# Where split weights and the parts of four combinations begin in SBUF: multiples of 128 bytes, or 8 to 112 bytes past one

## The chip, the cores and the metric

One core of one Trainium2 chip runs the whole program. The metric is the device time of one execution in microseconds (us).

## The reference

A trunk of two layers on 512 tokens of width 1024. Layer 0 mixes with multi-head latent attention (MLA), layer 1 with gated linear attention (GLA); an MLP follows each.

```python
for i in range(DEPTH):                      # DEPTH = 2
    xn = rms_norm(x, norm_mix[i])
    mix = mla_mixer(xn, ...) if i % 2 == 0 else gla_mixer(xn, ...)
    x = x + mix
    x = x + sq_relu_mlp(rms_norm(x, norm_mlp[i]), mlp_w_up[i], mlp_w_down[i])
return rms_norm(x, final_norm)

def sq_relu_mlp(xn, w_up, w_down):          # (512,1024) x (1024,4096) x (4096,1024)
    return jnp.square(jax.nn.relu(xn @ w_up)) @ w_down
```

MLA projects x to low-rank latents, from these to 8 heads of queries, keys and values, and applies causal softmax attention. GLA projects to queries, keys, values and gates and runs a chunked recurrence with a data-dependent decay. All data are float32.

## The kernel before, in words

Each float32 operand of a product is split in two: a high part, rounded to the type `float32r` by a copy on ACT, and a low part, the rest, by a subtraction on DVE (`split`, L104 and L107). A product of two split operands is then three matmuls: high by high, high by low, low by high (`mm3`, L112 to L114). A TensorE matmul has a stationary operand, at most 128 columns that are loaded ahead of it (LDWEIGHTS, PEld in the profile), and a moving one, here mostly 256 or 512 columns that stream through.

Weights come from HBM on SP's queue into tiles called `wraw` (in the MLP also `comb`), two in turn. `piece` splits one into a pair of tiles `wh` and `wl`, of which there are three each in turn, each of at most 1024 floats per partition. Both tags are used for two more tiles, `w_kr` in MLA and `wa` in GLA. All these come from one pool `sb`, whose tiles lie in SBUF one behind the other in the order of their first use: `wraw`, `wh`, `wl`, the sets A and B (split activations), `tmp` and more. Ahead of it lies the pool `const`, with the gains, the residual `xT` and small tables. Behind it the stages open pools of their own, among them `fast` for the MLP. Two tiles are wider than their contents: `gains` has 176 floats for 87, `rtok` 48 for 4. With these widths every tile of the `wh`, `wl`, A, B and `fast` tags begins at a multiple of 512 bytes. The residual tiles begin 64 bytes past a multiple of 128.

The MLP (`mlp`) is done by blocks of 512 hidden columns. The first block goes through plain three-term products. The other seven are a scheme with seven products in place of eight, for `w_up` and for `w_down`: the activations and the weights are cut in quadrants, sums and differences of quadrants are formed, and results are added up. `quadrants` forms four combinations of activation quadrants once per MLP, T1 to T4, and splits each into a tile of 4 x 2 x 256 floats: for each of four k, the high and the low part. `step` does one block: seven up products (`up_product`, L936: stationary a split weight of 128 columns, moving a plain quadrant or a combination, 256 columns, 24 matmuls each) in turn with seven down products (`down_product`, L945: stationary the split hidden activations, moving a split weight of 512 columns, 12 matmuls each). Four of the seven up products of a block read a combination, three a plain quadrant, which is a slice of set A. Two MLPs with seven such blocks make 14 steps. A product begins when its weight is split; a `wh` or `wl` tile is written again three splits later.

In the other stages `a_type`, `b_type` and `out_start` call `mm3` with a split weight as the stationary or the moving operand. The order of instructions on an engine is that of the program text, apart from a few marked places; none of these is near the change.

Of the kernel before, what the change touches and what calls it, by code (L numbers as in the profile page):

```python
# [10 lines left out]
F32 = mybir.dt.float32  # L11
F32R = mybir.dt.float32r
# [6 lines left out]
P = 128  # L19
D = 1024  # L20
S = 512
NT = S // P
ND = D // P
FF = 4096
FB = 512
TH = S // 2
MH = 8
NOPE = 128
ROPE = 64
# [6 lines left out]
RANK = 16  # L36
# [14 lines left out]
def trunk_kernel(ctx: ExitStack, tc: tile.TileContext, t_in: dict, out: bass.AP):  # L51
# [3 lines left out]
    const = ctx.enter_context(tc.tile_pool(name="const", bufs=1))  # L55
    sb = ctx.enter_context(tc.tile_pool(name="sb", bufs=1))
    count = [0]

    def uname(s):
        count[0] += 1  # L60
        return f"{s}_{count[0]}"
# [14 lines left out]
    def bank(tag):  # L76
        return psum["pool"].tile([P, 512], F32, tag=f"ps_{tag}", bufs=psum["banks"][tag], name=uname("ps"))
# [24 lines left out]
    def split(src, hi, lo, hi_eng=ACT, lo_eng=DVE, order=lambda i: i):  # L102
        if hi_eng is ACT:
            order(ACT.activation(hi, src, AF.Copy))  # L104
        else:
            hi_eng.tensor_copy(hi, src)
        lo_eng.tensor_tensor(lo, src, f(hi), ALU.subtract)  # L107
# [30 lines left out]
    def load(src, a, n):  # L138
        raw = sb.tile([P, a, n], F32, tag="wraw", bufs=2, name=uname("wraw"))
        SP.dma_start(raw, src)  # L140
        return raw

    def piece(raw, a, n, order=lambda i: i):
        hi = sb.tile([P, a, n], F32R, tag="wh", bufs=3, name=uname("wh"))
        lo = sb.tile([P, a, n], F32R, tag="wl", bufs=3, name=uname("wl"))
        split(raw, hi, lo, order=order)
        return hi, lo

    def cut(pair, *idx):
        return tuple(t[idx] for t in pair)  # L150
# [2 lines left out]
    rope_es = ExitStack()  # L153
    rk = rope_es.enter_context(tc.tile_pool(name="rope_keep", bufs=1, reuse_waits="tile"))

    gains_room = const.tile([P, 176], F32, name="gains")
    gains = gains_room[:, : N_GAIN + NT + 32]
    pos_i = gains[:, N_GAIN : N_GAIN + NT].bitcast(I32)
    invf = gains[:, N_GAIN + NT :]
# [38 lines left out]
    def gcol(name, j):  # L198
        c = GAIN_COL[name] + j
        return gains[:, c : c + 1]  # L200
# [166 lines left out]
    def col_chunk(w2d, c0, n):  # L367
        return load(w2d[:, c0 : c0 + n].rearrange("(k p) n -> p k n", p=P), w2d.shape[0] // P, n)


    def mla(layer, nrm, first, pools):
# [36 lines left out]
        KH = ND // 2  # L408
        raw = sb.tile([P, ND, 256], F32, tag="wraw", bufs=2, name=uname("wraw"))
        wq = []  # L410
        for h in range(2):
            ks = slice(h * KH, (h + 1) * KH)
            SP.dma_start(raw[:, ks], w_in[:, :256].rearrange("(k p) n -> p k n", p=P)[:, ks])
            wq.append(piece(raw[:, ks], KH, 256))
        for j in range(2):
            p = bank("c")
# [10 lines left out]

        raw = col_chunk(w_in, 256, P)
        w = piece(raw, ND, P)
        p = bank("b")  # L430
        a_type(p, w, X)
# [2 lines left out]


        raw = col_chunk(w_in, QL + KL, ROPE)
        wr = sb.tile([P, ND, 2, ROPE], F32R, tag="wh", bufs=3, name="w_kr")
        ACT.activation(wr[:, :, 1, :], raw, AF.Copy)
        DVE.tensor_tensor(wr[:, :, 0, :], raw, f(wr[:, :, 1, :]), ALU.subtract)
        p = bank("b")  # L440
# [24 lines left out]
        for k in range(2):  # L465
            SP.dma_start(raw[:, k], w_ukv[:, k, :, NOPE:])
        wv = [piece(raw[:, k : k + 1].rearrange("p a h c -> p a (h c)"), 1, D) for k in range(2)]
        V = [[None, None] for _ in range(NT)]
        VP = []
# [13 lines left out]
        for t in range(NT):  # L483
            tk = slice(t * P, (t + 1) * P)
            for hf in range(2):
                p = bank("bc"[hf])
# [15 lines left out]
            if t == 1:  # L502
# [3 lines left out]
                for j in range(2):  # L506
                    y = tmp()
                    DVE.scalar_tensor_tensor(y, pkv[j], gcol("kvn", 2 * layer + j), r_kv, ALU.mult, ALU.mult)
                    hi, lo = (keep.tile([P, S], F32R, tag=f"ckv{j}{x}", name=f"ckv{j}{x}") for x in "hl")
# [22 lines left out]
        wa = piece(raw3[:, 0:2], 2, 512)  # L532
        wq = [cut(wa, slice(None), 0), cut(wa, slice(None), 1), wb]
        qs = []
        for t in range(NT):
            tk = slice(t * P, (t + 1) * P)
            p = bank("b")
# [70 lines left out]
        p = bank("c")[:ROPE]  # L608
# [187 lines left out]
    def mlp(layer, nrm, nxt=None):  # L796
# [3 lines left out]
        KH = ND // 2  # L800
        first, second = slice(0, TH), slice(TH, S)
        es = ExitStack()
        fast = es.enter_context(tc.tile_pool(name=f"fast{layer}", bufs=1, reuse_waits="tile"))
# [11 lines left out]
        def comb(i):  # L815
            return fast.tile([P, 2 * S], F32, tag=f"comb{i}", bufs=1, name=uname("comb"))

        def by_k(t, n):
            return t.rearrange("p (k n) -> p k n", k=n)
# [4 lines left out]
        def signed(src, hi, lo, sign):  # L824
            ACT.activation(hi, src, AF.Copy, scale=sign)
            DVE.scalar_tensor_tensor(lo, src, sign, f(hi), ALU.mult, ALU.subtract)
# [34 lines left out]
        def quadrants():  # L861
            lead, trail = range(KH), range(KH, ND)
            quad["11"] = [nrm.parts[k][:, :, first] for k in lead]
            quad["21"] = [nrm.parts[k][:, :, first] for k in trail]
            quad["22"] = [nrm.parts[k][:, :, second] for k in trail]
            t1, t2, t3, t4 = (by_k(comb(i), KH) for i in range(2, 6))
            for k in lead:
                g1, g2 = (gcol(nrm.g, nrm.g0 + j) for j in (k, k + KH))
                u, v = xT[k], xT[k + KH]
                ACT.activation(t3[:, k], u[:, second], AF.Copy, scale=g1)  # L870
                DVE.scalar_tensor_tensor(t3[:, k], v[:, second], g2, t3[:, k], ALU.mult, ALU.subtract)
                DVE.scalar_tensor_tensor(t2[:, k], u[:, first], g1, t3[:, k], ALU.mult, ALU.add)
                DVE.scalar_tensor_tensor(t4[:, k], v[:, first], g2, t2[:, k], ALU.mult, ALU.subtract)
                DVE.scalar_tensor_tensor(t1[:, k], v[:, second], g2, t2[:, k], ALU.mult, ALU.subtract)
            for name, t, sign in (("T2", t2, -1.0), ("T3", t3, 1.0), ("T1", t1, -1.0), ("T4", t4, -1.0)):
                parts = fast.tile([P, KH, 2, TH], F32R, tag=name, name=uname(name))
                signed(t, parts[:, :, 0], parts[:, :, 1], sign)
                quad[name] = [parts[:, k] for k in lead]

# [163 lines left out]

        up_first(Q[0])
        quadrants()
        if not nxt:
            residual()
# [58 lines left out]
        if nxt:  # L1106
            room = [parts_room[(turn[0] + k) % 4] for k in range(4)]
# [5 lines left out]
            for c in range(2):  # L1113
# [10 lines left out]
                for j, p in enumerate(ps_):  # L1124
                    if j % 2 == 0:
                        w = piece(last_raw[c][:, :, j * P : (j + 2) * P], 4, 256)
                    for k in range(4):
                        wh, wl = cut(w, slice(None), k, slice(j % 2 * P, (j % 2 + 1) * P))
# [65 lines left out]
    def gla(layer, nrm, vtag, ytag):  # L1194
# [82 lines left out]

        own = tmp((P, NT, P))
        DVE.tensor_tensor(own, nrm.rstd.rearrange("p (t c) -> p t c", t=NT), ident.unsqueeze(1).to_broadcast([P, NT, P]), ALU.mult)
        rtok = sb.tile([P, 48], F32, tag="rtok", name="rtok")[:, :NT]  # L1280
        DVE.reduce_sum(rtok, own, AX.X)


# [1 line left out]
        raw = tmp((P, ND, RANK))  # L1285
        ACT.dma_start(raw, w_in[:, 2 * DK + 2 * D :].rearrange("(k p) n -> p k n", p=P))
        R2 = 2 * RANK
        wa = sb.tile([P, ND, 3, 2, RANK], F32R, tag="wl", bufs=3, name="wa")
        raw3 = raw.unsqueeze(2).to_broadcast([P, ND, 3, RANK])
        ACT.activation(wa[:, :, :, 1, :], raw3, AF.Copy)  # L1290
        DVE.tensor_tensor(wa[:, :, :, 0, :], raw3, f(wa[:, :, :, 1, :]), ALU.subtract)
# [6 lines left out]
        p = bank("a")  # L1298
# [361 lines left out]
    turns = rope_turns()  # L1660

    O, begun = mla(0, nrm, w0, mla_pools)
    rope_es.close()
    n_mlp0 = Norm(ND, inv_dr, "mlp", 0)
# [17 lines left out]
    mlp(0, n_mlp0, n_mix1)  # L1682
    psum_layout(False)
    Y, begun = gla(0, n_mix1, "B", "B")
    n_mlp1 = Norm(ND, inv_dr, "mlp", ND)
    out_proj(t_in["gla_w_o"][0], Y, n_mlp1, begun)
# [23 lines left out]
def build(nc, shapes):  # L1710
    args = {}
    for name, (shape, dt) in shapes.items():
        args[name] = nc.dram_tensor(f"in_{name}_dram", shape, dt, kind="ExternalInput").ap()
    o = nc.dram_tensor("out_0_dram", (S, D), F32, kind="ExternalOutput").ap()
    with tile.TileContext(nc) as tc:
        trunk_kernel(tc, args, o)
# [22 lines left out]
```

## Time and profile before

| | |
|---|---|
| median of 3 runs | 1061.13 us (1060.65 to 1061.31) |
| profiled execution | 1061.1 us |
| its span, first to last instruction | 1059.4 us |
| TensorE (PE) busy | 1049.3 us, 99% of the span, 5966 matmuls |
| weight loads (PEld) busy | 918.3 us, 87% |
| DVE busy | 876.1 us, 83% |
| ACT busy | 698.4 us, 66% |
| POOL busy | 113.3 us, 11% |

The page gives the busy time of each engine, the chain of work that ended last, and the costliest groups of instructions by source line, with count, mean and what ended the idle time before them. In a group, `ps<-wh,set` means that the moving operand is `wh` and the stationary one `set`. The duration of a matmul there has a modelled end and is longer than the distance from one matmul to the next; that distance is read from the chain in order of time, where `2.87 PE ps L936 x24` says that 24 matmuls took 2.87 us from the first start to the next piece.

### The profile page before, as it was taken

The numbers are of one execution on the slowest core, as the hardware profiler recorded it, in microseconds if no ns is written. First come the engines' busy times: TensorE is split into PE (matmuls) and PEld (weight loads), VectorE is DVE, ScalarE is ACT, GpSimd is POOL, SyncE is SP. The second block draws the span as 40 slices with busy tenths as digits, with TensorE's granted clock in tenths as the row PEclk, the third lists the DMA queues.
The fourth block names the chain that finished last, engine by engine and source line by source line (L and its number), as shares of the span: only waits on it lengthen the run. The fifth ranks groups of instructions, "written<-read, shape, count | busy, mean of one in ns | idle before, by whom it ended". The sixth has DMA issues, their size and how long they took to land.

```text
span 1059.4 us, 15597 instructions
## 1 busy us (share of the span) xinstructions
PE 1049.3 (99%) x5966; PEld 918.3 (87%) x5966; DVE 876.1 (83%) x1339; ACT 698.4 (66%) x1074; POOL 113.3 (11%) x128
## 2 busy tenths in 40 slices
PE   9999999999999999999999999999999999999997
PEld 7888888889999999998888888878899999999985
DVE  7899977979889889888686498469889989989993
ACT  7667654577767767766345565665567777777784
POOL 7410011101101111000000000000011010010000
PEclk9999999999999999999999999999999999999999
DMA  7311234765976875842322221434486696696622
GB/s 230 90 50 41 80 95 144 238 180 146 232 189 146 223 198 142 218 151 88 90 80 80 80 80 60 120 100 136 114 239 142 173 252 144 173 246 146 168 81 80
DMA packets 120492, 149.97 MB, mean 142 GB/s; under 512 B 9344, under 2 KB 86144, under 8 KB 120288
## 3 DMA queue, kind: packets, MB, share of 16 engines
q1 hardware_dynamic: 95920, 117.76, 34.5%
q0 software_dynamic: 22400, 29.36, 17.5%
q10 hardware_dynamic: 2096, 1.84, 0.6%
q8 instruction: 47, 0.77, 0.3%
q14 instruction: 29, 0.24, 0.1%
HBM read 144.49 MB, written 4.19 MB: 140 GB/s over the span
## 4 chain that ended last, share of the span: by engine, by line
PE 96%; DVE 2%; ACT 2%; issue 0%; DMA 0%; ACTq 0%; SPq 0%; DVEq 0%
PE ps L936 26%; PE ps L945 25%; PE ps L112 11%; PE ps L114 11%; PE ps L113 10%; PE ps L1130 2%; PE ps L1385 2%; PE ps L135 1%; PE ps L1165 1%; PE ps L405 1%; PE ps L1512 1%; DVE wl L107 0%; PE ps L668 0%; PE ps L1435 0%; PE ps L664 0%
## 5 line engine op out<-in xcount | busy, mean ns | idle before, releaser
L945 PE MATMUL ps<-wh,set 128*128 128x512 f32 x784 | 258.7, 391 | 0.0
L107 DVE TENSOR_TENSOR wl<-wraw,wh 128x1024 fp32r<-128x1024 f32 x139 | 169.5, 1222 | 40.8 <-ACT wh L104 40.5
L104 ACT ACTIVATE wh<-wraw 128x1024 fp32r<-128x1024 f32 x139 | 145.9, 1053 | 82.3 <-PE ps L113 38.9
L945 PEld LDWEIGHTS ps<-wh,set 128*128 128x128 f32 x784 | 147.5, 188 | 28.7
L936 PE MATMUL ps<-T,wh 128*128 128x256 f32 x896 | 163.5, 283 | 0.0
L104 ACT ACTIVATE wh<-comb 128x1024 fp32r<-128x1024 f32 x112 | 118.7, 1060 | 67.4 <-PE ps L936 43.7
L945 PE MATMUL ps<-wl,set 128*128 128x512 f32 x392 | 153.7, 392 | 0.0
L107 DVE TENSOR_TENSOR wl<-comb,wh 128x1024 fp32r<-128x1024 f32 x112 | 136.8, 1221 | 20.4 <-ACT wh L104 19.4
L936 PEld LDWEIGHTS ps<-T,wh 128*128 128x128 f32 x896 | 143.3, 191 | 4.5
L936 PE MATMUL ps<-T,wl 128*128 128x256 f32 x448 | 127.0, 283 | 1.0 <-DVE wl L107 1.0
L936 PE MATMUL ps<-set,wh 128*128 128x256 f32 x672 | 122.6, 283 | 0.0
L936 PEld LDWEIGHTS ps<-set,wh 128*128 128x128 f32 x672 | 107.4, 191 | 3.2
L112 PE MATMUL ps<-set,wh 128*128 128x512 f32 x280 | 109.4, 392 | 0.6 <-ACT set L1554 0.3
L113 PE MATMUL ps<-set,wh 128*128 128x512 f32 x280 | 109.5, 392 | 0.0
L114 PE MATMUL ps<-set,wl 128*128 128x512 f32 x280 | 109.0, 390 | 0.0
L936 PE MATMUL ps<-set,wl 128*128 128x256 f32 x336 | 95.2, 283 | 0.0
L936 PEld LDWEIGHTS ps<-T,wl 128*128 128x128 f32 x448 | 85.8, 191 | 1.5 <-DVE wl L107 1.4
L945 PEld LDWEIGHTS ps<-wl,set 128*128 128x128 f32 x392 | 74.0, 189 | 11.6
L925 POOL DMA_DIRECT2D comb<-in_mlp_w_down_dram x28 | 33.7, 1204 | 423.9 <-DMA comb<-in_mlp_w_down_dram 145.4
L936 PEld LDWEIGHTS ps<-set,wl 128*128 128x128 f32 x336 | 64.3, 191 | 0.0
L112 PEld LDWEIGHTS ps<-set,wh 128*128 128x128 f32 x280 | 52.5, 188 | 12.7 <-ACT wh L104 0.9
L104 ACT ACTIVATE set<-set 128x512 fp32r<-128x512 f32 (+1 forms) x70 | 41.9, 603 | 31.4 <-PE ps L945 29.4
(395 smaller groups left out, 2034.9 us busy)
## 6 DMA issues: line engine op xcount, KB each, us to landing
comb<-in_mlp_w_down_dram SPq DMA_DIRECT2D x74, 512.0 KB, 5.2
wraw<-in_mlp_w_up_dram SPq DMA_DIRECT2D x32, 1024.0 KB, 6.2
comb<-in_mlp_w_down_dram POOLq DMA_DIRECT2D x28, 512.0 KB, 8.1
wraw<-in_gla_w_in_dram SPq DMA_DIRECT2D x12, 1024.0 KB, 5.2
comb<-in_mlp_w_up_dram SPq DMA_DIRECT2D x14, 512.0 KB, 3.6
comb<-in_mlp_w_up_dram POOLq DMA_DIRECT2D x14, 512.0 KB, 8.9
wraw<-in_mlp_w_up_dram POOLq DMA_DIRECT2D x14, 512.0 KB, 7.3
wraw<-in_mla_w_o_dram SPq DMA_DIRECT2D x4, 1024.0 KB, 4.7
```

The source lines that it names most:

```text
L104: order(ACT.activation(hi, src, AF.Copy))
L107: lo_eng.tensor_tensor(lo, src, f(hi), ALU.subtract)
L112: PE.matmul(psum, wh, xh, start=start, stop=False)
L113: PE.matmul(psum, wh, xl, start=False, stop=False)
L114: PE.matmul(psum, wl, xh, start=False, stop=stop)
L135: PE.transpose(psum, src, ident[: src.shape[0], : src.shape[0]])
L405: PE.matmul(p, w[:, i, j * P : (j + 1) * P], x, start=start, stop=stop)
L925: POOL.dma_start(t, q(b, *more), accum_op=ALU.add)
L936: PE.matmul(o, a_, x_, start=start and j == 0 and k == 0 and n == 0, stop=k == KH - 1 and n == 2, skip_group_check=True)
L945: PE.matmul(o, x_, w_, start=start and k == 0 and n == 0, stop=k == 1 and n == 2, skip_group_check=True)
L1130: PE.matmul(p, a, x, start=False, stop=k == 3 and n == 2, skip_group_check=True)
L1385: PE.matmul(p[:, t - t0], k[:, t * P : (t + 1) * P], moving[:, t], start=True, stop=True)
```

## The change

`wh` and `wl` tiles grow by 32 floats, and the weight in them begins 0, 2 or 4 floats (0, 8 or 16 bytes) from the tile's start, by a count of the tiles that the tag has handed out. `w_kr` and `wa` are taken in the same way. Each combination's tile grows by 32 floats too, and its parts begin 12 (T2), 4 (T3), 20 (T1) or 28 (T4) floats from its start: 48, 16, 80 and 112 bytes. The widths of `gains` and `rtok` fall to 112 and 16 floats, 256 and 128 bytes less per partition. The tiles themselves begin at multiples of 128 bytes, of 512 no longer everywhere: sets A and B still do. No instruction is added, removed or moved.

```diff
+    taken = {"wh": 0, "wl": 0}
+
+    def weight_room(tag, a, n):
+        first = 2 * (taken[tag] % 3)
+        taken[tag] += 1
+        t = sb.tile([P, 2 * S + 32], F32R, tag=tag, bufs=3, name=uname(tag))
+        return t[:, first : first + a * n].rearrange("p (a n) -> p a n", a=a)
+
     def piece(raw, a, n, order=lambda i: i):
-        hi = sb.tile([P, a, n], F32R, tag="wh", bufs=3, name=uname("wh"))
-        lo = sb.tile([P, a, n], F32R, tag="wl", bufs=3, name=uname("wl"))
+        hi, lo = (weight_room(tag, a, n) for tag in ("wh", "wl"))
         split(raw, hi, lo, order=order)
         return hi, lo
...
-    gains_room = const.tile([P, 176], F32, name="gains")
+    gains_room = const.tile([P, 112], F32, name="gains")
...
-        wr = sb.tile([P, ND, 2, ROPE], F32R, tag="wh", bufs=3, name="w_kr")
+        wr = weight_room("wh", ND, 2 * ROPE).rearrange("p k (r c) -> p k r c", r=2)
...
             for name, t, sign in (("T2", t2, -1.0), ("T3", t3, 1.0), ("T1", t1, -1.0), ("T4", t4, -1.0)):
-                parts = fast.tile([P, KH, 2, TH], F32R, tag=name, name=uname(name))
+                at = {"T2": 12, "T3": 4, "T1": 20, "T4": 28}[name]
+                room = fast.tile([P, KH * S + 32], F32R, tag=name, name=uname(name))
+                parts = room[:, at : at + KH * S].rearrange("p (k a t) -> p k a t", k=KH, a=2)
                 signed(t, parts[:, :, 0], parts[:, :, 1], sign)
...
-        rtok = sb.tile([P, 48], F32, tag="rtok", name="rtok")[:, :NT]
+        rtok = sb.tile([P, 16], F32, tag="rtok", name="rtok")[:, :NT]
...
-        wa = sb.tile([P, ND, 3, 2, RANK], F32R, tag="wl", bufs=3, name="wa")
+        wa = weight_room("wl", ND, 6 * RANK).rearrange("p k (r a c) -> p k r a c", r=3, a=2)
```

## The prediction

> **What bounds the kernel now.** I read the page first (busy time, then the chain that ended last), then the chain in order of time around one step of the MLP, then the engines' busy time over that step.
>
> ```profile
> PE 1049.3 (99%) x5966; PEld 918.3 (87%) x5966; DVE 876.1 (83%) x1339; ACT 698.4 (66%) x1074; POOL 113.3 (11%) x128
> PEclk9999999999999999999999999999999999999999
> PE 96%; DVE 2%; ACT 2%; issue 0%; DMA 0%; ACTq 0%; SPq 0%; DVEq 0%
> PE ps L936 26%; PE ps L945 25%; PE ps L112 11%; PE ps L114 11%; PE ps L113 10%; PE ps L1130 2%; PE ps L1385 2%; PE ps L135 1%; PE ps L1165 1%; PE ps L405 1%; PE ps L1512 1%; DVE wl L107 0%; PE ps L668 0%; PE ps L1435 0%; PE ps L664 0%
> ```
>
> TensorE at its full granted clock carries 96% of the chain, and almost all of that are matmuls that read a split weight: the up products (`up_product`, L936), the down products (`down_product`, L945) and the three-term products (`mm3`, L112 to L114). Transfers, ACT and DVE hold it up for 4% in all. So this change, which adds and removes no instruction, can only matter through the pace of matmuls or of the splits that feed them. That a PE is busy says nothing of its pace; the chain in order of time does, because it counts matmuls from start to start.
>
> ```profile
> 481.50 1.75 PE ps L1123 x16
> 495.92 10.89 PE ps L1130 x48
> 867.95 2.87 PE ps L936 x24
> 870.82 2.75 PE ps L945 x12
> 873.57 2.87 PE ps L936 x24
> 876.44 2.75 PE ps L945 x12
> ```
>
> One up product of 24 matmuls with 256 columns takes 2.87 us, 119.6 ns each, whether its moving operand is a combination T or a plain quadrant. 48 matmuls with 512 columns take 10.89 us, 226.9 ns each. The difference, 107.3 ns for 256 columns, gives 0.419 ns per column, and so 12.3 ns of each matmul that columns don't explain: 119.6 - 107.3 = 12.3, and 226.9 - 214.6 = 12.3 too. There are no gaps between the pieces of the chain (867.95 + 2.87 = 870.82). The fixed 12.3 ns is therefore the only thing on TensorE's side that a shift of addresses could take away or enlarge. The 16 transposes of L1123 load 128 columns of weights each and stream 128: 109.4 ns each, so a weight load alone can turn over every 109.4 ns.
>
> **The change part by part.** The matmuls concerned, from the groups that keep shapes apart:
>
> ```profile
> L936 PE MATMUL ps<-T,wh 128*128 128x256 f32 x896 | 163.5, 283 | 0.0
> L936 PE MATMUL ps<-T,wl 128*128 128x256 f32 x448 | 127.0, 283 | 1.0 <-DVE wl L107 1.0
> L936 PE MATMUL ps<-set,wh 128*128 128x256 f32 x672 | 122.6, 283 | 0.0
> L936 PE MATMUL ps<-set,wl 128*128 128x256 f32 x336 | 95.2, 283 | 0.0
> L945 PE MATMUL ps<-wh,set 128*128 128x512 f32 x784 | 258.7, 391 | 0.0
> L945 PE MATMUL ps<-wl,set 128*128 128x512 f32 x392 | 153.7, 392 | 0.0
> L112 PE MATMUL ps<-set,wh 128*128 128x512 f32 x280 | 109.4, 392 | 0.6 <-ACT set L1554 0.3 <-DVE xT L781 0.2
> L112 PE MATMUL ps<-wh,set 128*128 128x512 f32 x144 | 58.6, 407 | 0.0
> ```
>
> The first operand named is the one that streams. So 896 + 448 = 1344 matmuls stream a combination's part, which now begins 48, 16, 80 or 112 bytes past a multiple of 128; all 672 + 336 + 1344 = 2352 up products load a split weight; 784 + 392 = 1176 down products stream one; and of the three-term products 3 x 280 load one and 3 x 144 stream one (the two L112 rows stand for L113 and L114, which have the same counts).
>
> *The parts of the combinations.* In before every operand of an up product begins at a multiple of 128, the streamed one and the loaded one start together at each matmul, and each matmul pays the same 12.3 ns. Afterwards the streamed T begins at another place in the 128 bytes than the weight that is loaded beside it, in all 1344. No row of before shows such a pair, so the cost is bounded: above by nothing saved (119.6 stays), below by the whole fixed part gone, 1344 x 12.3 ns = 16.5 us. The weight loads would allow that: they turn over in 109.4 ns in L1123. I take half, 6.15 ns each, 8.3 us, since nothing says which of the two ends is nearer. The Trainium skill has a figure for the same thing: TensorE: Matmul & The Clock Gate, section Back-to-back issue gap, gives a warm gap of N / 2.4 + 2.5 ns, which is 109.2 ns for 256 columns and 215.8 for 512. The trace disagrees by 10.4 and 11.1 ns; an estimate by that page, with its gap reached in the T products alone, would be 1344 x 10.4 ns = 14.0 us saved.
>
> *The split weights.* Two of three tiles now begin 8 or 16 bytes past a multiple of 128. The nearest rows for an address off 128 are the transposes of the residual, whose stationary tiles begin 64 bytes past one:
>
> ```profile
> L135 PEld LDWEIGHTS ps<-ident,g 128*128 128x128 f32 x32 | 3.8, 140 | 0.9 <-DVE set L1555 0.3
> L1123 PEld LDWEIGHTS ps<-ident,xT 128*128 128x128 f32 x32 | 3.6, 141 | 0.3
> L235 ACT ACTIVATE tmp<-xT 128x512 f32<-128x512 f32 x28 | 16.7, 623 | 0.0
> L123 ACT ACTIVATE tmp<-tmp 128x512 f32<-128x512 f32 x7 | 4.4, 629 | 0.2
> ```
>
> A load from 64 bytes past takes 141 ns against 140 from a multiple of 128, and an ACT read from there 623 against 629. I take nothing for the weights, neither gain nor loss. The bounds come from other rows. As a gain, they could take the same fixed part out of the matmuls with an undisturbed T or 512 columns; I leave that as the low end. As a loss, see the rivals.
>
> *The splits.* DVE writes and ACT writes now go to those shifted tiles. Cover for a dearer split is the slack of one step:
>
> ```profile
> core 0: us, PE busy (x) PEld busy (x) DVE busy (x) ACT busy (x) POOL busy (x), PEclk, DMA share, GB/s
> 867.95:907.29 39.34, 39.34 (x254) 35.90 (x254) 34.90 (x39) 28.38 (x35) 5.81 (x5) 1.00 0.74 189
> L107 DVE TENSOR_TENSOR wl<-comb,wh 128x1024 fp32r<-128x1024 f32 x112 | 136.8, 1221 | 20.4 <-ACT wh L104 19.4
> ```
>
> DVE is busy 34.90 of 39.34 us, so 4.44 us per step are free; a step has 14 splits on DVE, and each of 1221 ns could take 300 ns more before DVE became the bound. The gain forecast, 96 T matmuls per step x 6.15 ns = 0.59 us, uses little of the same slack, so what is late next is still TensorE. Nothing is queued differently: the two pads cut (256 and 128 bytes) hold no data, buffer counts and the order on every queue stay, and no wait is added.
>
> *Sum.* The profiled execution took 1061.1 us, 1.7 more than its span of 1059.4, and the median of the runs shown is 1061.13, so the same. 1061.1 - 8.3 = 1052.8 us.
>
> **The rivals.** *No change (1061.1 us).* If the 12.3 ns are a fixed cost of handing over from one weight to the next, addresses don't enter. For it: the same 12.3 ns with 256 and 512 columns, and with streamed or loaded weights. Against it: the pace is not that rigid, as the rows below show. The Trainium skill is on its side: SBUF — State Buffer, Who interferes with whom, says that TensorE has two independent read ports, one for streaming and one for weights, and waits on nobody; by that rule two operands of one matmul can't disturb each other wherever they begin. No row of before tests this.
>
> *One more line per read (slower, 1065.8 us).* A tile that begins 8 bytes past a multiple of 16 may need one more fetch of 16 bytes per read. A third of the split tiles are such. Price by rows: a streamed read loses 4 columns, 4 x 0.419 = 1.7 ns, in a third of 1176 + 432 matmuls, 0.9 us; a loaded read loses 4 of its 128 columns, 4 x 109.4 / 128 = 3.4 ns, in a third of 2352 + 840, 3.6 us at most; with 0.2 us for the 64 + 32 + 32 + 16 = 144 matmuls of L1130 and L405 (rows below), 4.7 us. It decides only if the T parts save less than that.
>
> ```profile
> L1130 PE MATMUL ps<-set,wh 128*128 128x512 f32 x64 | 19.9, 392 | 0.0
> L1130 PE MATMUL ps<-set,wl 128*128 128x512 f32 x32 | 12.5, 390 | 0.0
> L405 PE MATMUL ps<-set,wh 128*128 128x512 f32 x32 | 9.0, 397 | 0.4 <-ACT set L246 0.4
> L405 PE MATMUL ps<-set,wl 128*128 128x512 f32 x16 | 4.9, 390 | 0.0
> ```
>
> The Trainium skill, SBUF — State Buffer, Door 1: The DMA port swizzle, has such lines: 16 bytes, with a penalty for each access that crosses to a new one. No row of before shows it: the equal times at 64 bytes past don't test it, since 64 is a multiple of 16.
>
> *An unsettled pace (slower, up to 1082 us).* The one stretch of before where a split tile is not read at steps of 512 bytes is L1301 and L1302 (steps of 384 in a `wl` tile):
>
> ```profile
> 524.35 0.23 PE ps L1301
> 524.58 0.24 PE ps L1302
> ...
> 527.60 0.23 PE ps L1301
> 527.83 0.24 PE ps L1302
> ```
>
> 16 matmuls take 527.83 + 0.24 - 524.35 = 3.72 us, 232.5 ns each instead of 226.9, 5.6 ns more, though their weights have fewer columns. If reads that no longer begin alike never settle at the pace of the uniform ones, this falls on all matmuls with an operand off 128: 1344 with T, two thirds of the other 1008 up products and of 1176 + 840 + 432 + 144 with 512 columns, 3744 x 5.6 ns = 21.0 us. For it: the settled pace is the low end of what the rows show. Against it: those 16 have tiles of 96 columns, which may be the cause alone. It begins to decide where 8.3 / 0.0056 = 1480 of those 3744 matmuls lose that much while T gains as forecast.
>
> **How the numbers follow.** The forecast has 0.50, no change 0.10, one more line 0.24, the unsettled pace 0.16. About 0.2%, 2.1 us, is what a measurement can tell from no change; the forecast and only it lies beyond that on the fast side, so faster 0.50, same 0.10, slower 0.40. The forecast's own range is 1044.6 (the whole fixed part gone from T) to 1059. The range for 8 in 10 goes from 1041, with a little saved on the weights too, to 1076, which takes in the one more line and the smaller part of the unsettled pace; it leaves out about 0.06 below and 0.11 above.
>
> **What would show it.** Right: in the chain in order of time an up product with T takes about 2.72 us for its 24 matmuls, one with a plain quadrant stays at 2.87, a down product stays at 2.75, a step falls from 39.34 to about 38.75 us with DVE's 34.90 unchanged, and the counts of all groups stay. Wrong: the T products stay at 2.87 us (no change), the plain up products or L945 move away from 2.87 and 2.75 (the weights matter), pieces of 12 down matmuls grow towards 2.82 (unsettled pace), or DVE's 1221 ns grow and DVE shows up in the chain.

## The result, and the profile after

The changed kernel takes 1068.25 us, median of 3 runs (1067.87 to 1068.35), against 1061.13: 1.0067 times, 95% interval 1.0044 to 1.009. It is slower by 7.1 us, where 8.3 us less had been forecast. The page after, in the lines that answer to those of before:

```profile
PE 1056.4 (99%) x5966; PEld 916.0 (86%) x5966; DVE 876.1 (82%) x1339; ACT 698.5 (65%) x1074; POOL 113.4 (11%) x128
PEclk9999999999999999999999999999999999999999
PE 96%; ACT 1%; DVE 1%; DMA 0%; issue 0%; ACTq 0%; SPq 0%; DVEq 0%
```

TensorE holds the same 96% of the chain at the same granted clock, with as many matmuls, and is busy 7.1 us longer. No other engine's share of the chain grew, and DVE's 876.1 us are the same to the tenth. The whole difference is pace. The chain in order of time, with the source lines moved by nine (the up product is L945 now, the down product L954, L1130 is L1139):

```profile
486.34 11.13 PE ps L1139 x48
872.25 2.79 PE ps L954 x12
875.04 2.85 PE ps L945 x24
877.88 2.77 PE ps L954 x12
880.66 2.84 PE ps L945 x24
883.50 2.81 PE ps L954 x12
891.93 2.76 PE ps L945 x24
```

Two things move in opposite directions. A piece of 24 products with 256 columns takes 2.76 to 2.85 us instead of 2.87. A piece of 12 with 512 columns takes 2.77 to 2.81 instead of 2.75, and the 48 of L1139 take 11.13 us where they took 10.89: 231.9 ns each against 226.9. Before, the pieces of a kind were equal within 0.01 us; after, they differ by about 0.1 us.

The groups that keep shapes apart say the same:

```profile
L954 PE MATMUL ps<-wh,set 128*128 128x512 f32 x784 | 261.7, 395 | 0.0
L945 PE MATMUL ps<-T,wh 128*128 128x256 f32 x896 | 161.3, 280 | 0.0
L945 PE MATMUL ps<-T,wl 128*128 128x256 f32 x448 | 125.9, 281 | 1.1 <-DVE wl L107 1.1
L945 PE MATMUL ps<-set,wh 128*128 128x256 f32 x672 | 121.3, 281 | 0.0
L113 PE MATMUL ps<-set,wh 128*128 128x512 f32 x280 | 110.7, 396 | 0.0
L107 DVE TENSOR_TENSOR wl<-comb,wh 128x1024 fp32r<-128x1024 f32 x112 | 136.6, 1219 | 19.5 <-ACT wh L104 17.5 <-DMA comb<-in_mlp_w_down_dram 1.5
```

The mean duration of a matmul has a modelled end, but it moves with the pace: from 391 to 395 ns where the distance from start to start grew by 4 ns, from 283 to 280 or 281 where it shrank by 2. The plain up products (`set,wh`) gained as the T products did, although their moving operand had stayed where it was; their stationary one, the weight, had moved.

In the rest of the text the *pitch* is the mean distance from one matmul's start to the next one's, over the pairs of a group that follow each other without a break. It is worked out from all the starts in the trace, in ns; the last column is the sum over the counts of the prediction:

| stationary or moving weight, columns | matmuls | before | after | difference, us |
|---|---|---|---|---|
| moving weight, 512 (down products, part of `mm3`) | 1608 | 229.0 | 232.6 | +5.7 |
| stationary weight, 512 (rest of `mm3`, L1139, L412) | 984 | 227.3 | 232.2 | +4.8 |
| stationary weight, plain moving, 256 | 1008 | 119.7 | 118.3 | -1.3 |
| stationary weight, T moving, 256 | 1344 | 119.7 | 118.0 | -2.2 |

The sum is +7.0 us of the 7.1 measured. These are means. Before, the twelve distances from the first matmul of a down piece to the next piece are 233, 236, 228, 232 and 231 ns in the mean and then seven of 226.7: five matmuls pass before the pace settles, and the mean is 229.0.

### The profile page after: what moved, and what is told of

It is laid out like the page before. It is cut to its first block, busy times and chain, and to the rows that moved or that the text cites. A ratio compares the mean times of both kernels' runs of the same rounds, so it can differ in the third digit from the quotient of the medians.

```text
span 1066.5 us, 15597 instructions
## 1 busy us (share of the span) xinstructions
PE 1056.4 (99%) x5966; PEld 916.0 (86%) x5966; DVE 876.1 (82%) x1339; ACT 698.5 (65%) x1074; POOL 113.4 (11%) x128
## 4 chain that ended last, share of the span: by engine, by line
PE 96%; ACT 1%; DVE 1%; DMA 0%; issue 0%; ACTq 0%; SPq 0%; DVEq 0%
PE ps L954 26%; PE ps L945 26%; PE ps L112 11%; PE ps L114 11%; PE ps L113 11%; PE ps L1139 2%; PE ps L1394 2%; PE ps L135 1%; PE ps L1174 1%; PE ps L412 1%; PE ps L1521 1%; PE ps L675 0%; PE ps L1444 0%; PE ps L671 0%; PE ps L674 0%; DMA gains<-in_gains_dram 0%
## 5 line engine op out<-in xcount | busy, mean ns | idle before, releaser
L954 PE MATMUL ps<-wh,set 128*128 128x512 f32 x784 | 261.7, 395 | 0.0
L107 DVE TENSOR_TENSOR wl<-wraw,wh 128x1024 fp32r<-128x1024 f32 x139 | 169.4, 1221 | 41.8 <-ACT wh L104 41.6
L954 PEld LDWEIGHTS ps<-wh,set 128*128 128x128 f32 x784 | 147.5, 188 | 30.0
L104 ACT ACTIVATE wh<-comb 128x1024 fp32r<-128x1024 f32 x112 | 118.8, 1061 | 65.6 <-PE ps L945 41.7
L945 PE MATMUL ps<-T,wh 128*128 128x256 f32 x896 | 161.3, 280 | 0.0
L954 PE MATMUL ps<-wl,set 128*128 128x512 f32 x392 | 154.6, 394 | 0.0
L107 DVE TENSOR_TENSOR wl<-comb,wh 128x1024 fp32r<-128x1024 f32 x112 | 136.6, 1219 | 19.5 <-ACT wh L104 17.5
L945 PEld LDWEIGHTS ps<-T,wh 128*128 128x128 f32 x896 | 141.2, 188 | 5.0
L945 PE MATMUL ps<-T,wl 128*128 128x256 f32 x448 | 125.9, 281 | 1.1 <-DVE wl L107 1.1
L945 PE MATMUL ps<-set,wh 128*128 128x256 f32 x672 | 121.3, 281 | 0.0
L112 PE MATMUL ps<-set,wh 128*128 128x512 f32 x280 | 110.7, 397 | 0.5 <-ACT set L1563 0.3
L113 PE MATMUL ps<-set,wh 128*128 128x512 f32 x280 | 110.7, 396 | 0.0
L945 PEld LDWEIGHTS ps<-set,wh 128*128 128x128 f32 x672 | 105.8, 188 | 3.6
L945 PE MATMUL ps<-set,wl 128*128 128x256 f32 x336 | 94.5, 281 | 0.0
L945 PEld LDWEIGHTS ps<-T,wl 128*128 128x128 f32 x448 | 84.4, 188 | 1.6 <-DVE wl L107 1.5
L954 PEld LDWEIGHTS ps<-wl,set 128*128 128x128 f32 x392 | 73.9, 189 | 13.1
L114 PEld LDWEIGHTS ps<-set,wl 128*128 128x128 f32 x280 | 52.7, 188 | 12.5 <-DVE wl L107 0.4
L945 PEld LDWEIGHTS ps<-set,wl 128*128 128x128 f32 x336 | 63.2, 188 | 0.0
```

Of the source, the lines that this page charges most:

```text
L112: PE.matmul(psum, wh, xh, start=start, stop=False)
L113: PE.matmul(psum, wh, xl, start=False, stop=False)
L114: PE.matmul(psum, wl, xh, start=False, stop=stop)
L945: PE.matmul(o, a_, x_, start=start and j == 0 and k == 0 and n == 0, stop=k == KH - 1 and n == 2, skip_group_check=True)
L954: PE.matmul(o, x_, w_, start=start and k == 0 and n == 0, stop=k == 1 and n == 2, skip_group_check=True)
```

## The experiments

Theory A is that the pitch of a matmul depends on the pair of places at which its moving and its stationary operand begin. Its rivals were that only single operands off some step (16, 32 or 128 bytes) cost time, and that the loss lies in what else the change moves: the pads, the place of all tiles, the order of the parts.

**A probe of pairs of starts.** It computes nothing of the reference: two nested loops over 14 moving and 14 stationary tiles, 24 equal matmuls for each pair, first with 512 columns, then with 256, and no other engine at work. (`SS` is the same list as `MS`.)

```python
for n in (512, 256):
    for o in MS:            # 0 8 16 32 48 64 80 96 112 128 192 256 320 384 bytes past 512
        for q in SS:
            for _ in range(REPS):    # 24
                PE.matmul(acc[:, :n], still[q], moving[o][:, :n], start=True, stop=True)
```

> This kernel computes nothing of the reference: it runs groups of 24 equal matmuls, one group for each pair of starts (moving operand 0 to 384 bytes past a multiple of 512, stationary operand the same), with 512 and with 256 columns. Theory A (the pace depends on where the two operands begin relative to each other in 512 bytes): about 227 ns at 512 columns and 120 ns at 256 only where both begin alike, 230 to 236 ns elsewhere at 512 and 115 to 119 at 256. Theory B (only a start off a multiple of 128 matters): all pairs of 0, 128, 256 and 384 run at 227 and 120. Theory C (the pace of a long uniform run does not depend on the starts at all, and only changes from one matmul to the next disturb it): 227 and 120 everywhere.

The steady pitch within the groups of 24, without the first eight distances of each:

| moving, stationary start | 0, 0 | 64, 64 | 128, 0 | 0, 128 | 0, 8 | 0, 16 | 16, 0 | 8, 8 | 112, 0 | 192, 0 |
|---|---|---|---|---|---|---|---|---|---|---|
| 512 columns | 226.7 | 226.7 | 233.6 | 233.7 | 230.7 | 233.5 | 231.5 | 231.1 | 231.1 | 233.5 |
| 256 columns | 120.0 | 120.0 | 118.7 | 120.0 | 115.5 | 118.2 | 116.8 | 120.0 | 113.3 | 113.3 |

(The 512-column entry at 0, 0 is that of 256, 0, whose row is that of 0 everywhere else: the first group runs while the clock still rises.) The groups of this run show it in their means, moving operand named first:

```profile
L41 PE MATMUL acc<-m64x,s64x 128*128 128x512 f32 x24 | 5.6, 390 | 0.0
L41 PE MATMUL acc<-m320x,s320x 128*128 128x512 f32 x24 | 5.6, 390 | 0.0
L41 PE MATMUL acc<-m128x,s0x 128*128 128x512 f32 x24 | 5.8, 395 | 0.0
L41 PE MATMUL acc<-m0x,s128x 128*128 128x512 f32 x24 | 5.8, 395 | 0.0
L41 PE MATMUL acc<-m0x,s8x 128*128 128x512 f32 x24 | 5.7, 393 | 0.0
```

Four readings. Both starts count together: with 512 columns, moving either operand alone by 128 bytes costs 6.9 or 7.0 ns, and moving both costs nothing (226.7).

With 512 columns equal starts at a multiple of 32 give 226.7 ns, the lowest of all 196 pairs; some unequal pairs reach it too, and 142 of the 196 stand at 230 to 237. With 256 columns the same equal starts give 120.0, and the lowest pitch is 113.3, half of 226.7. So a settled product of 512 columns was at the floor already in the layout of before, and one of 256 columns stood 6.3 ns above its own.

Starts that are 256 bytes apart mostly do alike: a moving start of 256 gives what 0 gives in every pair. It is no exact rule. Of the 114 pairs that the probe holds more than once when starts are taken modulo 256, 18 differ by about 0.5 ns or more, most of them where the stationary start is the one that is 256 further. The widest, with 512 columns, is 226.7 ns at 112, 128 and 236.5 at 112, 384. Such pairs also stand behind other groups in the run, so whether the place or what ran before makes the difference isn't separated here.

A start at 8 bytes is cheaper than one at 16 as the stationary start (230.7 against 233.5 ns with 512 columns) and dearer as the moving one (233.2 against 231.5), the other start being 0. So steps of 16 bytes give no rule here.

Of the expectations, Theory A came nearest, with two misses: the step is nearer to 256 bytes than to 512, and some unequal pairs are as fast as equal ones. Theories B and C fell.

**The change without the 8 and 16 bytes.** The rooms stay as wide as in the change, so that `wh` and `wl` buffers still begin at different multiples of 128; the weight begins at its tile's start.

```diff
-        first = 2 * (taken[tag] % 3)
+        first = 0
```

> The changed kernel with the weights back at the start of their tiles, so at multiples of 128 that are 0, 128, 256 or 384 past a multiple of 512; the T parts stay shifted. Theory A (512 bytes count): still slow, 1064 to 1068 us, 512-column products at 230 ns or more. Theory B (128 bytes count): 512-column products back at 227 to 229 ns, 1058 to 1061 us.

1065.7 us, 1.0042 of before (1.0027 to 1.0057). 2.5 us come back, no more. The 512-column products stand at 231.2 ns in the mean with a moving weight and with a stationary one. So most of the loss was not in the 8 and 16 bytes, but in the 128 bytes by which the wider buffers shift each other: every second one begins 128 past a multiple of 256.

**The parts of the combinations alone.**

```diff
-                parts = fast.tile([P, KH, 2, TH], F32R, tag=name, name=uname(name))
+                at = {"T2": 12, "T3": 4, "T1": 20, "T4": 28}[name]
+                room = fast.tile([P, KH * S + 128], F32R, tag=name, name=uname(name))
+                parts = room[:, at : at + KH * S].rearrange("p (k a t) -> p k a t", k=KH, a=2)
```

> The kernel before with the T parts alone shifted by 48, 16, 80 and 112 bytes from multiples of 512. Theory A: T products at 116 to 119 ns, about 1344 x 2 ns = 2.7 us saved, plain up products at 120 and down products at 228 to 230 as before: 1058 to 1059.5 us. Theory C (changes disturb): down products get slower too, 1061 to 1064 us.

1058.91 us, 0.9978 of before (0.9968 to 0.9988): faster than both kernels. The four starts are worth very different amounts: 119.6 to 119.7 ns at 80 bytes, 118.4 to 118.9 at 48 and at 16, 115.2 and 114.5 at 112. The means of the other products stay as before, within 0.1 ns. The weights therefore cost about 1068.25 - 1058.91 = 9.3 us in the changed kernel. The subtraction isn't quite pure: there the combinations' tiles begin at other multiples of 128, so that T2 and T1 begin at 176 and 208 modulo 256 and not at 48 and 80. But the T products go at 118.0 ns there and at 117.9 here, and the three other rows of the table above add up to 9.2 us.

**Everything behind the gains shifted by 256 bytes.**

```diff
-    gains_room = const.tile([P, 176], F32, name="gains")
+    gains_room = const.tile([P, 112], F32, name="gains")
```

> The kernel before with the gains' pad cut by 256 bytes, so that weights, sets and the stages' pools all begin 256 past a multiple of 512, alike. If it is the starts relative to each other that count: no change, 1061 us. If it is the place in SBUF: slower, 1065 us or more.

1061.25 us, 1.0001 (0.9991 to 1.001). Neither the narrower pad nor a common shift by 256 matters.

**The weights alone, at 0, 8 or 16 past a multiple of 256.** One tile holds six blocks of 1024 floats. The two lines that follow are those of the first form; the second adds an offset there for the five pieces of the opening.

```diff
+        first = (2 * i + (tag == "wl")) * 2 * S + (0, 2, 4)[i]
+        return split_room["t"][:, first : first + a * n].rearrange("p (a n) -> p a n", a=a)
```

> The kernel before with only the split weights moved: the eighteen data blocks begin 0, 8 or 16 bytes past a multiple of 256, while the split sets and the four combinations' parts stay at multiples of 512. Theory A (the pitch of a pair of products follows from the two operands' starts relative to each other, modulo 256 bytes; prices from the probe): about 2016 products of 512 columns pair a weight at 8 or 16 with a set at 0 and lose some 3.7 ns each over 227, with 432 more in the lines of pass B, so about 9.1 us lost; products of 256 columns of the same pairs gain about 2.1 ns each, 2352 of them, so 4.9 us won; the sum is about 1065.5 us. If 256-column products do not gain in the real order, 1070 us. Theory 'as the prediction had it' (the weights' starts cost nothing): 1061 us. Theory 'the loss is in the new order of the parts alone': 1061 us too.

> The weights alone at 0, 8 or 16 past a multiple of 256 again. In the first form the five pieces of the opening were written over each other: twelve products of the opening took the wrong block, and the first product came 4.4 us later than in the kernel before (20.74 against 16.38 us in the traces). Here the five pieces have places of their own and nothing is left out. Theory A: the products themselves cost what the first form's trace shows (512 columns 230.8 to 231.8 ns against 227.4 to 229.8, 256 columns 118.0 against 119.5 to 120), so the time is the first form's 1071.2 less the late start, 1066 to 1067 us. The theory that the split weights' starts cost nothing: 1061 us.

The first form gave 1071.19 us and the second 1064.5, 1.003 of before (1.0019 to 1.0042), 3.7 us more than its 1060.8. Only the second can be compared: beside its late start the first ran at a mean granted clock of 0.995, the second at 0.999. The first expectation of 1065.5 was 1.0 us high, and the second, which took only the late start off the first form, 1.5 to 2.5. By pitch: moving weights 229.0 to 231.8 in 1608 matmuls, +4.4 us; stationary ones 227.3 to 230.9 in 984, +3.5; 256 columns 119.7 to 118.0 in 2352, -3.9: together +4.0 us, 3.7 measured. This loss and the one of the 128 bytes (1065.7 - 1058.91 = 6.8 us) add up to 10.5 us, not to the 9.3 of both, so they aren't independent.

**The weights alone, all 128 past a multiple of 256**, with `(32, 32, 32)` in place of `(0, 2, 4)`.

> The kernel before with all split weights moved alike, 128 bytes past a multiple of 256; sets and combinations stay at multiples of 512. All the weights' starts are still multiples of 128, so a rule that only counts whole steps of 128, 64 or 32 bytes sees nothing here: such a rule says 1061 us. Theory A (relative start modulo 256 bytes; prices from the probe's pairs 0 with 128 and 128 with 0: 233.3 ns at 512 columns against 226.7, 120.2 at 256 against 120.0): 2592 products of 512 columns lose 6.6 ns each, 17 us, and the 256-column ones stay, so about 1078 us. If the real order with its parts of three weights softens the loss as it does in the changed kernel (4 to 5 ns), 1071 to 1074 us.

> All weights 128 past a multiple of 256 again, with places of their own for the five pieces of the opening; nothing is left out. Theory A: the first form's 1076.6 less its late start of 4.4, so about 1072 us: 2592 products of 512 columns lose 4 to 5 ns each (232.4 to 232.8 against 227.4 to 229.8) and those of 256 columns stay near 119.2. A rule that counts whole steps of 128 bytes says 1061 us.

1076.55 us in the first form, 1070.26 in the second, 1.0084 (1.007 to 1.0098), 1.7 less than expected. This is the run that decides against a rule by steps: every weight stands at a multiple of 128, and so of 16 too, and the loss is larger than with 8 and 16. The groups of the second form, one tile for both halves:

```profile
L957 PE MATMUL ps<-w_split,set 128*128 128x512 f32 x1176 | 290.1, 395 | 0.0
L948 PE MATMUL ps<-set,w_split 128*128 128x256 f32 x1008 | 127.3, 282 | 0.0
L113 PE MATMUL ps<-set,w_split 128*128 128x512 f32 x280 | 110.8, 396 | 0.0
```

By pitch: +3.6 ns in 1608, +5.4 in 984, -0.5 in 2352, together +9.9 us, 9.5 measured.

**All four parts at 192 bytes**, where the probe has 113.4 ns.

```diff
-                parts = fast.tile([P, KH, 2, TH], F32R, tag=name, name=uname(name))
+                room = fast.tile([P, KH * S + 64], F32R, tag=name, name=uname(name))
+                parts = room[:, 48 : 48 + KH * S].rearrange("p (k a t) -> p k a t", k=KH, a=2)
```

> The kernel before with the four combinations' parts all at 192 bytes past a multiple of 512; weights and sets stay at multiples of 512. Theory A (relative start modulo 256; the probe has 113.4 ns for a moving start of 192 and a stationary start of 0 at 256 columns, against 120.0): 1344 products gain 6.6 ns each, 8.9 us, so about 1052 us. If the gain belongs to equal products in a row and a real order keeps half of it, 1056 to 1057 us. Theory 'only differences between the four parts matter' (all alike, so nothing): 1061 us.

1056.93 us, 0.9963 (0.9949 to 0.9976), 4.2 us less than before's 1061.14. That meets the expectation of 1056 to 1057, but in part by luck. The T products stand at 117.2 to 118.3 ns, not at 113.4, and save 2.6 us, less than a third of the 8.9. About 1.5 us more come from where none had been expected, the down products, although neither of their operands had moved:

```profile
875.78 2.87 PE ps L937 x24
878.66 2.75 PE ps L946 x12
881.40 2.83 PE ps L937 x24
884.23 2.72 PE ps L946 x12
886.95 2.83 PE ps L937 x24
889.78 2.72 PE ps L946 x12
```

A down piece behind a plain up product keeps 2.75 us and its slow start of five. The 56 behind a T product go at 227 ns from the first matmul on and take 27 ns less each. So what runs before a product counts too.

**The changed kernel's own starts in a probe**, triples of products as `mm3` has them, high, high and low half in turn, and a scan of the moving start.

> A probe that computes nothing of the reference: groups of 48 products, as 16 triples over three moving and three stationary tiles whose starts are those of the changed kernel (high halves 0, 136 and 16 past a multiple of 256, low halves 128, 8 and 144, combinations' parts 176, 16, 208 and 112, plain parts 0), then a scan of the moving start from 0 to 240 in steps of 16 with the stationary start at 0. Theory A with prices that add by pair: 512-column triples with the high halves average 230 to 232 ns and with the low halves 231 to 233 ns against 226.7 for plain parts; 256-column triples with plain parts 117 to 119 against 120; the combinations 113 to 120 according to their starts. If a triple's pitch is set by the change from one product to the next instead (each unequal neighbour disturbs the one behind it), the triples lie 2 ns or more above the mean of their pairs. The scan should show the lowest 256-column pitch near 113.3 at starts of 112 or 192 and the 512-column one never below 226.7.

Averaged over the six pairings of high and low halves, with the changed kernel's groups beside them: 512 columns with a stationary weight 231.8 (232.2 in the kernel), with a moving one 230.7 (232.6), 256 columns with plain parts 118.5 (118.3), and T2, T3, T1 and T4 118.1, 116.9, 118.0 and 118.8 (117.4, 117.9, 118.0, 118.6). So TensorE alone, with every other engine idle, reproduces the pace within 2 ns. Single triples range from 226.7 to 233.3 and from 113.3 to 120.0, and a triple isn't always the mean of its pairs. With the high half at 0 and the low half at 128 the pairs give (226.7 + 226.7 + 233.7) / 3 = 229.0 ns; as stationary operands such a triple has 231.1, as moving ones 228.9. So neither of the two rules in the expectation holds for every triple. Nor is a pair's own pitch fixed: with 512 columns the pair 128, 0 has 233.6 ns in the first probe and 232.5 in this one. The scan with the stationary start at 0, lowest and highest row, and the row of 192:

```profile
L42 PE MATMUL acc<-at0x,plain 128*128 128x256 f32 x48 | 5.9, 283 | 0.0
L42 PE MATMUL acc<-at192x,plain 128*128 128x256 f32 x48 | 5.6, 276 | 0.0
L42 PE MATMUL acc<-at112x,plain 128*128 128x256 f32 x48 | 5.6, 275 | 0.0
```

**All four parts at 112 bytes**, with 28 in place of 48.

> The kernel before with all four combinations' parts at 112 bytes past a multiple of 256, weights and sets at multiples of 512. The one combination that stood at 112 in the run of the parts alone went at 114.5 to 115.2 ns, against 119.5 to 120 before and 117.5 for all parts at 192. Theory A with prices from the real order: 1344 products gain 4.8 ns each, 6.4 us, so about 1054.7 us. If that combination's gain came from its place in the order (its neighbours at other starts) and not from its start, all at 112 give what all at 192 gave, 1057 us, or less.

1054.73 us (1054.34 to 1055.21), 0.9937 (0.9923 to 0.995): the fastest form, 6.1 us below before and 13.5 below the change. Its groups and its chain:

```profile
L946 PE MATMUL ps<-wh,set 128*128 128x512 f32 x784 | 258.8, 391 | 0.0
L937 PE MATMUL ps<-T,wh 128*128 128x256 f32 x896 | 157.5, 277 | 0.0
L937 PE MATMUL ps<-T,wl 128*128 128x256 f32 x448 | 124.1, 277 | 1.0 <-DVE wl L107 1.0
L937 PE MATMUL ps<-set,wh 128*128 128x256 f32 x672 | 122.6, 283 | 0.0
```

```profile
874.97 2.87 PE ps L937 x24
877.84 2.75 PE ps L946 x12
880.59 2.76 PE ps L937 x24
883.35 2.75 PE ps L946 x12
886.10 2.76 PE ps L937 x24
```

A product with T takes 2.76 us, one with a plain quadrant keeps 2.87, and the down products keep 2.75 or, in a few places, 2.76. All four parts go at 114.6 to 115.3 ns, so the gain of T4 belonged to its start and not to its place in the order. 1344 x 4.6 ns = 6.2 us.

## Why the prediction was wrong

*The bound* was right: TensorE's pace decides, with 96% of the chain before and after.

*The split weights taken as nothing* is the step that failed. The runs show about +9.3 us in its place, more than the whole gain that was forecast. The rows chosen as nearest were durations of transposes' weight loads and of ACT reads (141 against 140 ns, 623 against 629). They say how long one access of one operand takes, and the effect isn't there: it is in the distance between two matmuls, and it depends on the pair of operands. A row that did show it was in the prediction already, under the rivals: the 16 matmuls of L1301 and L1302, whose stationary tile is read at steps of 384 bytes, that is at 0 and 128 modulo 256 in turn, stood at 232.5 ns (231.8 by the trace's starts, without the last piece, which no matmul follows). The probe's pair of a stationary start at 128 and a moving one at 0 has 233.7 with 512 columns, and half such pairs would give 230.2. So the starts explain most of that row without the 96 columns that were held against it; whether these add the rest isn't shown. The row should have carried the term.

*The unsettled pace* was thus the right rival in kind, with the chance too low (0.16) and the size too high (21.0 us). After the change the twelve distances of a down piece stand at 231.6 to 233.2 ns in the mean, and none settles at 226.7. The size was too high because 2016 of its 3744 matmuls have 256 columns and became faster, not slower. In the others its 5.6 ns were 3.6 to 4.9. It also counted only two thirds of the weights, those at 8 and 16; of the third at 0 the low halves lose too, because their tiles begin 128 off.

*The T parts*, 8.3 us, were mis-sized: 2.1 us alone. The sign was right, and so was the idea that unequal starts can help a matmul with 256 columns. But half of the bounds' distance stood for four starts that are worth 0, 1, 1 and 5 ns in the real order. Only all four at 112 come near the forecast, at 6.1.

*The fixed 12.3 ns per matmul* was an artefact of fitting a line through two points, each taken at equal starts. The lowest pitches of the probe are 113.3 and 226.7 ns, in the ratio of the columns: 0.443 ns a column, and no fixed part is needed, though two widths alone can't prove that there is none. Before, settled 512-column products were at their floor, and only the slow starts of pieces could gain; the 256-column ones stood 6.3 ns above theirs. "The same 12.3 ns in both" looked like a confirmation and was none: it had been used up in finding two unknowns from two numbers.

*One more line per read* fell: the weights at 128 cross no line more and lose 9.5 us, the weights at 0, 8 and 16 lose 3.7, and in the probe a stationary start at 8, where this rival saw most of its cost, is cheaper than one at 16 (230.7 against 233.5 ns). That its 1065.8 us lie only 2.5 us below the result is luck. *No change* fell. The rule put beside it, from the Trainium skill (SBUF — State Buffer, Who interferes with whom), that TensorE's two read ports are independent, isn't what the times look like: with 512 columns, moving one operand's start by 128 bytes changes the pitch from 226.7 to 233.6 or 233.7 ns, and moving the other one too brings 226.7 back. Which part of TensorE waits isn't shown. The gap of N / 2.4 + 2.5 ns from the Trainium skill (TensorE: Matmul & The Clock Gate, Back-to-back issue gap), which that section calls the isolated gap of a single matmul, was not reached by any pair: 113.3 against 109.2, and 226.7 against 215.8.

*The splits on DVE and ACT* cost nothing, as forecast: 1219 ns against 1221, and 34.91 us busy in the same 39.34 us against 34.90.

```profile
867.95:907.29 39.34, 39.34 (x254) 35.66 (x253) 34.91 (x39) 28.40 (x35) 4.99 (x4) 1.00 0.74 188
```

*Open* is the mechanism: no run shows why the two starts set the pitch, nor by what path the products before a piece change its first five distances. Open too is why a moving start of 192 gives 113.3 ns where one product is repeated but 117.2 to 118.3 in the kernel, while 112 gives 113.3 and about 115. The kernel turns over stationary slices, moving slices and accumulators, and the probes turned over only some of these. And 256-column products with plain quadrants still go at 119.5 to 120 in the fastest form; their starts weren't moved, since they share set A with products of 512 columns.

## What to carry to other kernels

When TensorE is the bound, read its pitch by group, not its busy share, and compare groups of the same shape: two pitches for one shape are a lead. Here products of 512 columns ran best with both operands beginning alike, at multiples of 32 modulo 256 bytes, while products of 256 columns ran best with a chosen difference (112 bytes, of those tried in the kernel), so an operand that both kinds read is better left alone and one that only the short ones read can be moved. Widening buffers by 128 bytes shifts all that follow, and that cost more here (6.8 us) than the shifts of 8 and 16 bytes that were meant (2.5). A probe of one repeated product finds the candidates; only the real order of products gives the price.

## What the runs showed of the hardware that was not expected

A matmul's pitch depends on the starts of its two operands together, with no other engine at work: 226.7 to 236.9 ns with 512 columns, 113.3 to 122.7 with 256. The lowest values are in the ratio of the columns. Starts 256 bytes apart mostly do alike, with exceptions of up to 9.8 ns, and a common shift of nearly everything by 256 bytes does nothing (1.0001). Equal starts at multiples of 32 are alike, but equal starts at 8 aren't: 231.1 ns with 512 columns. The products before count as well: with T at 192 bytes the down pieces behind T products, themselves unmoved, lost their slow start (233, 236, 228, 232 and 231 ns became 227).
